# Feed-forward by Strassen's scheme: one of the seven gate and up products by a second level, the next weights asked for one tile earlier, own places for each kind of temporary

## The chip, the cores and the metric

The kernel runs on one core of one Trainium2 chip. The metric is the device time of one launch in microseconds (us); less is better. The core's engines each work through an instruction list of their own, in order: PE (TensorE, the matrix unit; its weight loads are listed apart as PEld), DVE (VectorE), ACT (ScalarE), POOL (GpSimd), and SP (SyncE), which here only asks for transfers (DMA). Engines wait for one another by semaphores. All data are float32. PE multiplies float32 words of reduced precision, so each operand is split into a high and a low word, and one product of two operands is three matmuls (high·high, high·low, low·high).

## The reference, cut to what matters

One layer (BATCH 1, SEQ 2048, D_MODEL 1024, D_FF 2816). The change touches only the last three lines:

```python
h = h + einsum(concat([fox, pool]), w_out)          # attention and pooling
h = h + einsum(mo, w_mem_out)                       # memory cross-attention
hn = rmsnorm(h, g_ffn[l])
gu = jnp.einsum('bsd,df->bsf', hn, w_gate_up[l])    # 1024 -> 2 * 2816
act = jax.nn.silu(gu[..., :D_FF]) * gu[..., D_FF:]
h = h + jnp.einsum('bsf,fd->bsd', act, w_down[l])   # 2816 -> 1024
```

## The kernel before, in words

The feed-forward part runs in two passes (`ps_` = 0, 1) over 1024 tokens each; a pass is `gate_up`, then `down`. Tokens stand in blocks of 512 (`FT`), features in tiles of 128 (`NF` = 22 tiles).

`gate_up` makes, for one tile t, gate and up of 128 features for two blocks of 512 tokens. That is a product of 2 x 2 blocks (rows: the two halves of the 1024 inputs; columns: gate and up on one side, the two token blocks on the other), done by Strassen's scheme in Winograd's form with seven products: b11·x11, b21·x12, t2·s2, t1·s1, t3·s3 in the tile's own turn, t4·x22 and b22·s4 in the turn of tile t+1. One such product (`product`) is 4 slices of 128 inputs x 3 word products = 12 matmuls of 512 columns. They gather in three PSUM banks per tile (a, b, c: banks 0 to 2 or 3 to 5 in turn); banks 6 and 7 serve the four late token tiles (below). The sums t1 to t4 of the weights are made on DVE in `weight_steps`; its `put` makes a word pair, a cast on ACT for the high word and a subtraction on DVE (line 64, `sub_hi`) for the low word. Word pairs have eight places in a ring (`word_pair`). The x and s operands of the tokens are word pairs too: x11, x12, s2, s1 stand in slabs (their tiles appear as qs, kh, kl, cb), and s3, x22, s4 are made at the start of pass 0 by `put_late` from raw loads (`xr`).

`down` multiplies the 22 activation tiles by the down weights, again with seven products, of 11 steps each: 77 steps of 12 matmuls. It draws raw blocks through SP (`draw`), splits them into word pairs (`ww`), and after a product adds four banks to four residual blocks `o` (line 1612 before, 1722 after) and stores them through POOL (`out_dram`). While it runs in pass 0, `next_ops` at steps 20, 34, 48 and 62 makes the token operands of pass 1. The sums of the down weights are made in pass 0 of `gate_up` on POOL (`down_sums`, from loads `wdr`) and written to HBM. The sums of activations are made on POOL as well (`act_sums`). Four late token tiles are normed and turned inside pass 0 of `gate_up` (`late_tile`).

Order: in the feed-forward part PE and SP go through their instructions in the order in which the code is written (`in_order(EN.SP)`). The order on DVE, ACT and POOL is set by the framework's scheduler. Blocks of temporaries come from one pool of 14 places of 128 x 512 (`temp`), and a block waits until an older holder of its place is done with.

## Time and profile before

| | |
|---|---|
| time, median of 3 runs (lowest, highest) | 2487.02 us (2485.74, 2490.58) |
| profiled execution, its own time | 2486.17 us |
| its span in the trace | 2484.4 us |
| granted TensorE clock, mean | 0.999 |
| DMA, mean over the span | 173 GB/s |
| gate_up pass 0 / down pass 0 | 1219.98 to about 1638 / to about 1852 us |
| gate_up pass 1 / down pass 1 | to about 2266 / to the end |

The rows shown below are of four kinds. A row of busy time by stretch has, behind the stretch and its length, busy us and instruction count of PE, PEld, DVE, ACT and POOL, then the granted clock (1.00 is full), the DMA share and GB/s. A row of groups has line, engine, operation, output <- inputs, shapes and count, then busy us and the mean ns of one. A row of the timeline has start, duration (of the whole run of xN), engine, line, operation, and in brackets the idle time before it with what ended it. A row of transfers has queue, count, KB each and median us from the ask to the landing. Starts are us from the start of the span. A matmul's duration is its way through the unit; the next one starts earlier.

### The profile page before, as it was taken

What the parts mean: (1) busy time and instruction counts of PE and PEld (TensorE: products, weight loads), DVE (VectorE), ACT (ScalarE), POOL (GpSimd) and SP (SyncE); (2) the same over time, 40 slices, a digit from 0 to 9 for tenths busy, and PEclk for the clock granted to TensorE, in tenths of its full rate; (3) what the DMA queues carried; (4) which work ended last, traced back from release to release, by engine and by line L of the source; (5) the groups of instructions that cost most, each with busy time, mean ns of one, the idle gap of its engine ahead of it and who ended that gap; (6) DMA issues with size and microseconds to landing.
All of it is one profiled execution on the core that took longest, in us unless ns stands there. A gap on an engine that the chain in (4) does not pass through costs nothing.

```text
span 2484.4 us, 36567 instructions
## 1 busy us (share of the span) xinstructions
PE 2468.4 (99%) x12899; PEld 2109.2 (85%) x12899; DVE 1662.4 (67%) x3000; ACT 1204.0 (48%) x2308; POOL 745.1 (30%) x1012
## 2 busy tenths in 40 slices
PE   9999999999999899999999999999999999999999
PEld 8999989878888788888888888888888888888887
DVE  7444495489999855556868787667676666665554
ACT  6434341089999835445633433335443333333443
POOL 2223200045556524343135545430002222222000
PEclk9999999999999999999999999999999999999999
DMA  8665566476776443233645544467762333325666
GB/s 295 216 191 173 163 210 180 150 197 159 177 166 156 120 149 112 106 111 134 233 158 182 193 174 167 172 230 251 259 239 98 106 119 115 107 98 198 229 204 212
DMA packets 218279, 428.95 MB, mean 173 GB/s; under 512 B 25952, under 2 KB 101728, under 8 KB 207264
## 3 DMA queue, kind: packets, MB, share of 16 engines
q1 hardware_dynamic: 187920, 330.12, 42.4%
q0 software_dynamic: 30032, 96.23, 10.4%
q8 instruction: 102, 1.67, 0.3%
q14 instruction: 81, 0.66, 0.1%
q10 hardware_dynamic: 144, 0.26, 0.0%
HBM read 287.47 MB, written 134.61 MB: 170 GB/s over the span
## 4 chain that ended last, share of the span: by engine, by line
PE 83%; DVE 1%; issue 1%; POOL 1%; ACT 0%; DVEq 0%; POOLq 0%; ACTq 0%
PE bk L71 17%; PE bk L69 17%; PE bk L70 17%; PE acc L917 5%; PE sps L841 5%; PE tp L56 4%; PE mmps L69 4%; PE mmps L71 4%; PE mmps L70 4%; PE oo L69 1%; PE oo L70 1%; PE oo L71 1%; PE zp L71 1%; PE zp L69 1%; PE zp L70 1%
## 5 line engine op out<-in xcount | busy, mean ns | idle before, releaser
L64 DVE TENSOR_TENSOR ww<-draw,ww 128x512 fp32r<-128x512 f32 x308 | 209.7, 719 | 151.1 <-ACT ww L184 150.6
L184 ACT CAST ww<-draw 128x512 fp32r<-128x512 f32 x308 | 179.2, 620 | 220.9 <-PE bk L71 175.3
L64 DVE TENSOR_TENSOR ww<-graw,ww 128x512 fp32r<-128x512 f32 x220 | 174.3, 798 | 107.8 <-ACT ww L1137 107.6
L70 PE MATMUL bk<-ww,ww 128*128 128x512 f32 x619 | 240.2, 388 | 0.0
L71 PE MATMUL bk<-ww,ww 128*128 128x512 f32 x619 | 240.2, 388 | 0.0
L69 PE MATMUL bk<-ww,ww 128*128 128x512 f32 x619 | 240.1, 388 | 0.0
L1137 ACT CAST ww<-graw 128x512 fp32r<-128x512 f32 x220 | 136.0, 622 | 179.5 <-PE bk L71 164.4
L64 DVE TENSOR_TENSOR pl<-tp,ph 128x512 fp32r<-128x512 f32 (+3 forms) x298 | 177.5, 598 | 7.3 <-ACT ph L950 6.6
L69 PE MATMUL zps<-wh,xhi 128*128 128x384 f32 (+1 forms) x512 | 174.1, 340 | 0.0
L71 PE MATMUL zps<-wh,xl 128*128 128x384 f32 (+1 forms) x512 | 172.0, 336 | 0.0
L70 PE MATMUL zps<-wl,xhi 128*128 128x384 f32 (+1 forms) x512 | 171.9, 336 | 0.0
L950 ACT CAST ph<-tp 128x512 fp32r<-128x512 f32 (+3 forms) x298 | 152.7, 529 | 24.3 <-PE tp L56 22.9
L69 PE MATMUL bk<-qs,ww 128*128 128x512 f32 x352 | 137.8, 391 | 0.0
L71 PE MATMUL bk<-qs,ww 128*128 128x512 f32 x352 | 137.2, 390 | 0.1
L70 PE MATMUL bk<-kh,ww 128*128 128x512 f32 x352 | 136.9, 389 | 0.0
L69 PE MATMUL bk<-kl,ww 128*128 128x512 f32 x352 | 136.9, 389 | 0.0
L70 PE MATMUL bk<-cb,ww 128*128 128x512 f32 x352 | 136.9, 389 | 0.0
L71 PE MATMUL bk<-kl,ww 128*128 128x512 f32 x352 | 136.9, 389 | 0.0
L71 PEld LDWEIGHTS bk<-ww,ww 128*128 128x128 f32 x619 | 116.2, 188 | 24.1
L70 PEld LDWEIGHTS bk<-ww,ww 128*128 128x128 f32 x619 | 116.2, 188 | 24.0
L69 PEld LDWEIGHTS bk<-ww,ww 128*128 128x128 f32 x619 | 116.2, 188 | 23.7
L1615 POOL DMA_DIRECT2D out_dram<-o x31 | 16.7, 541 | 374.9 <-DVE o L1612 373.0
(641 smaller groups left out, 7066.1 us busy)
## 6 DMA issues: line engine op xcount, KB each, us to landing
graw<-in_w_gu_dram SPq DMA_DIRECT2D x44, 1024.0 KB, 5.6
draw<-in_w_down_dram SPq DMA_DIRECT2D x66, 256.0 KB, 4.4
xl<-in_xT_dram SPq DMA_DIRECT2D x64, 256.0 KB, 5.5
wdr<-in_w_down_dram SPq DMA_DIRECT2D x22, 512.0 KB, 4.3
xrow<-in_x_dram SPq DMA_DIRECT2D x16, 512.0 KB, 4.8
vd<-cb SPq DMA_DIRECT2D x16, 512.0 KB, 3.6
kh<-qkT1h SPq DMA_DIRECT2D x16, 512.0 KB, 10.3
kl<-qkT1l SPq DMA_DIRECT2D x16, 512.0 KB, 12.3
```

Source lines behind the costliest of these rows:

```text
L56: return pe.transpose(out.bitcast(F32R), src, identr[:])
L64: (eng or dve).tensor_tensor(out=lo, in0=src, in1=f(hi), op=ALU.subtract)
L69: pe.matmul(ps, lhsT=sh, rhs=mh, start=first, stop=False, skip_group_check=goes_on)
L70: pe.matmul(ps, lhsT=sh, rhs=ml, start=False, stop=False, skip_group_check=goes_on)
L71: pe.matmul(ps, lhsT=sl, rhs=mh, start=False, stop=last, skip_group_check=goes_on)
L184: act.copy(hi, raw)
L841: pe.matmul(ps[:, :w], lhsT=qs[:, i * P:(i + 1) * P], rhs=kk[:, cs], start=(a == 0), stop=(a == 1))
L917: pe.matmul(acc[:m, q0 * P:], lhsT=v[:, j, :m], rhs=(pl if low else ph)[:, q0 * P:], start=state["n"] == 1, stop=state["n"] == 2 * nk)
L950: act.copy(ph[:, sl], tp[:, sl])
L1137: needs(act.copy(quad(hi), v), *(tie if nm == "t2" else ()))
L1615: pool.dma_start(out[rows_, cs], o)
```

## The change

- Tiles t-1 and t (t odd) share their b21·x12 products. Both weights times x12 are one 2 x 2 block product again, done by the same scheme one level down: seven quarter products (`quarter`) of 2 slices x 3 words = 6 matmuls of 256 columns, so 42 matmuls of 256 in place of 24 of 512. They gather in bank 7 (`u`, used three times), and in halves of two c banks. DVE adds their results to `s0` and `s1` by six adds of 256 columns and one of 512, in place of two of 512.
- `weight_steps` of an odd tile takes the b21 of both tiles (`pair`, a load of its own) and makes the seven quarter weights h11 to ht4: four more subtractions of 256 columns, and `put_half` four times (three of 512, one of 256) in place of two `put` of b21.
- x12 becomes four blocks of word pairs for the quarters (`quarter_ops`): for pass 0 after the first copy out of the first tile, for pass 1 at step 68 of `down`. s3 takes the slab of x12.
- The weights of tile t+1 are asked for at the top of tile t. In tile 0, t1·s1 comes ahead of t2·s2.
- `temp` has places for each kind (`SETS`), and a double block `tw`, which raw x12, raw s4 and the loads of the down weights share. The four `o` blocks rotate through places 0 to 7; sums and half of raw x12 have places 7 and 8.
- `down_sums` moves from POOL to DVE, by half blocks (22 calls of 4 subtractions of 256 per block). The silu of the gate works in place in PSUM. Late tiles use bank 6 only.

```diff
@@ weight_steps
+        if pair is None:
+            t4 = b[1, 0]
+            sub(t4, b[1, 0], t2)
+        else:
+            t4 = b[0, 0]
+            sub(t4, b[1, 0], t2)
+            odd = b[1, 0]
+            put_half(pair, "h11", "h21")
+            both = sum_("ht")
+            sub(both[:, :2], odd[:, :2], pair[:, :2])
+            sub(both[:, 2:], odd[:, 2:], both[:, :2])
+            put_half(both, "ht1", "ht2")
+            sub(odd[:, :2], odd[:, 2:], odd[:, :2])
+            put_half(odd, "ht3", "h22")
+            sub(pair[:, 2:], pair[:, 2:], both[:, 2:])
+            put_half(pair[:, 2:], "ht4")
@@ the feed-forward part
-        temp = lambda n: fb.tile([P, FT], F32, tag="t", name=n, bufs=14)[:]
+        SETS = dict(s1=[0, 1], s2=[2, 3, 4], s3=[5, 6], sum=[7, 8], h2=[9], x22=[3, 4, 6, 9], o=list(range(8)))
+        def temp(name, kind):
+            SETS[kind].append(SETS[kind].pop(0))
+            n = SETS[kind][-1]
+            return fb.tile([P, FT], F32, tag=f"t{n}", name=name, bufs=1)[:]
+        def raws_of(op):
+            if op == "x22":
+                return [temp("xr", "x22") for _ in range(4)]
+            t_ = wide_temp("xr")
+            return [t_[:, :FT], t_[:, FT:], temp("xr", "sum"), temp("xr", "sum")]
+        def quarter_ops(raws, *after):
...
+            def put(t_, j, v):
+                needs(act.copy(t_[:, j], v), *after)
+                sub_hi(t_[:, 2 + j], v, t_[:, j])
+            for j in range(2):
+                r0, r1 = raws[j], raws[j + 2]
+                put(first_, j, r0[:, :B])
+                put(wide[0], j, r1)
+                tt(r1[:, B:], r0[:, B:], r1[:, B:], ALU.add)
+                tt(r0[:, B:], r0[:, :B], r0[:, B:], ALU.subtract)
+                tt(r0[:, :B], r1[:, B:], r0[:, :B], ALU.subtract)
+                tt(r1[:, :B], r1[:, :B], r0[:, :B], ALU.subtract)
+                put(wide[1], j, r1)
+                put(wide[2], j, r0)
@@ down_sums
-            sub = lambda o, p_, q_: pool.tensor_tensor(out=o, in0=p_, in1=q_, op=ALU.subtract)
+            sub = lambda o, p_, q_: dve.tensor_tensor(out=o, in0=p_, in1=q_, op=ALU.subtract)
@@ gate_up
+        def quarter(ps, wop, xop, first):
+            for j in range(2):
+                cs = slice(j * P, (j + 1) * P)
+                mm3(ps, (wop[0][:, cs], wop[1][:, cs]), quarters[xop][j], first and j == 0, j == 1, not first)
+                if odd:
+                    u, c0, c1 = bank(7)[:, :B], bank(3 * ((t + 1 + turned) % 2) + 2), c[:, B:]
+                    s0 = prev["s1"]
+                    quarter(u, w["h11"], "a11", True)
+                    quarter(c1, w["ht1"], "s1", True)
+                    quarter(c0[:, :B], w["h21"], "a12", True)
+                    add(s0[:, :B], u)
+                    add(s1[:, B:], c1)
...
-                if cur:
-                    product(c, w["b21"], "x12", True)
-                    dve.tensor_tensor(out=s1, in0=c, in1=s1, op=ALU.add)
-                    act.activation(s1, s1, AF.Silu)
-                    cur["s1"] = s1
-                else:
+                if odd:
+                    quarter(u, w["ht2"], "s2", False)
+                    quarter(c1, w["h22"], "s4", False)
+                    add(s1[:, :B], u)
+                    add(s1[:, :B], c1)
+                elif not cur:
                     next(follow)
...
+                if odd:
+                    quarter(u, w["ht3"], "s3", False)
+                    quarter(c0[:, B:], w["ht4"], "a22", True)
+                    add(s0[:, B:], u)
+                    add(s1[:, B:], u)
+                    add(s0, c0)
+                    for s_ in (s0, s1):
+                        act.activation(s_, s_, AF.Silu)
@@ the call
-            early = {(0, 2): [lambda: put_late("s3")], (0, 3): [lambda: put_late("x22")], (1, 1): [lambda: put_late("s4")]}
+            early = {(0, 2): [lambda: quarter_ops(late_raw["x12"], *emptied[:1])], (0, 3): [lambda: put_late("x22")],
+                     (1, 1): [last_op]}
+            def next_quarters():
+                raws = raws_of("x12")
+                for j in range(4):
+                    sp.dma_start(raws[j], hTd[2][j + 4])
+                quarter_ops(raws)
+                between[68] = [next_quarters]
```

The first place is DVE at the end of tile 0 of pass 0. Before, three operands stand between the last low word of x22 and the low word of tile 1's b11 (`ww7_15237`; `graw` is the raw weight tile, `t1` a sum of it):

```order
L64 TENSOR_TENSOR x22l2_15141<-xr_15106,x22h2_15140 128x512 [waits DMAHW0_49,Activation_49]
L64 TENSOR_TENSOR x22l3_15143<-xr_15107,x22h3_15142 128x512 [waits DMAHW1_49,Activation_49]
L64 TENSOR_TENSOR s4l1_15123<-xr_15113,s4h1_15122 128x512 [waits DMAHW3_49,DMASW6_49,Activation_49]
L1140 TENSOR_TENSOR t1_15243<-graw_15235 128x512 [waits DMAHW0_49]
L64 TENSOR_TENSOR s4l2_15125<-xr_15114,s4h2_15124 128x512 [waits DMASW5_49,DMAHW4_49,DVE_49,Activation_49]
L64 TENSOR_TENSOR ww7_15237<-graw_15235,ww7_15237 128x512 [waits Activation_49]
```

After, the same place on DVE; `x12q` to `x12q2` are the low words of x12's quarters, line 1509 makes their sums, and `ww6_15183` is the low word of tile 1's b11:

```order
L64 TENSOR_TENSOR x12q2_15106<-xr_15052,x12q2_15106 128x512 [waits Activation_49]
L1509 TENSOR_TENSOR xr_15052<-xr_15054,xr_15052 128x256 [waits DVE_49]
L64 TENSOR_TENSOR x12q1_15105<-xr_15053,x12q1_15105 128x512 [waits Activation_49]
L1509 TENSOR_TENSOR xr_15054<-xr_15054,xr_15052 128x256 [waits DVE_49]
L64 TENSOR_TENSOR x12q2_15106<-xr_15052,x12q2_15106 128x512 [waits Activation_49]
L64 TENSOR_TENSOR x22l0_15076<-xr_15059,x22h0_15075 128x512 [waits DMASW7_49,DMAHW6_49,DMASW6_49,DMASW5_49]
L64 TENSOR_TENSOR x12q1_15105<-xr_15054,x12q1_15105 128x512 [waits Activation_49]
L64 TENSOR_TENSOR x22l1_15078<-xr_15060,x22h1_15077 128x512 [waits DMAHW7_49,DMASW1_49]
L64 TENSOR_TENSOR x22l2_15080<-xr_15061,x22h2_15079 128x512 [waits DMAHW0_49,DMASW0_49]
L64 TENSOR_TENSOR x22l3_15082<-xr_15062,x22h3_15081 128x512 [waits DMAHW1_49,DMASW4_49]
L1683 TENSOR_TENSOR s3_15178<-bk1_15088,s3_15178 128x512 [waits PE_49]
L64 TENSOR_TENSOR ww6_15183<-graw_15083,ww6_15183 128x512 [waits DMAHW2_49,Activation_49]
```

Ahead of b11 of tile 1 now stand the whole of x12's quarters, the four low words of x22, and an add that waits for the last product of tile 0.

The second place is ACT over the same tile, after the change. `s1_15102` and `s2_15156` are the copies out of bank 0 behind b11 and behind t2; the rest are high words of x12's quarters:

```order
L1627 COPY s1_15102<-bk0_15087 128x512 [waits DMASW4_49,DMASW3_49,DMAHW4_49,DMASW1_49,PE_49]
L1512 CAST x12f_15107<-xr_15052 128x256 [waits DMAHW2_49,Activation_49]
L1512 CAST x12f_15107<-xr_15052 128x256 [waits DMAHW3_49]
L1512 CAST x12q_15104<-xr_15053 128x512 [waits DMAHW4_49,DVE_49]
L1676 COPY s2_15156<-bk0_15087 128x512 [waits PE_49]
L1512 CAST x12q_15104<-xr_15054 128x512 [waits DMAHW5_49]
```

The fourth cast of x12 stands behind a copy that waits for PE's third product of tile 0.

The third place is SP at the end of the sixth product of `down` in pass 0, where a step's two raw blocks (`draw`) are asked for in pairs. Before, the blocks of steps 66, 67 and 68 stand one behind the other:

```order
L1641 DMA draw_19980<-act1b1_11413 128x512 [waits DMAHW2_49,DMAHW3_49,DMAHW1_49,DMAHW4_49,DVE_49,Activation_49]
L1642 DMA draw_19980<-wt4k0_11499 128x512
L1641 DMA draw_19980<-act3b1_11421 128x512
L1642 DMA draw_19980<-wt4k1_11503 128x512
L1641 DMA draw_20021<-act5b1_11429 128x512 [waits DMAHW6_49,DMAHW5_49,DMAHW7_49,DMAHW0_49,DVE_49]
```

After, the four raw blocks of x12 stand between them:

```order
L1752 DMA draw_20381<-wt1_11497 128x512
L1807 DMA xr_20422<-hTd2_11406 128x512 [waits DMAHW2_49]
L1807 DMA xr_20422<-hTd2_11406 128x512 [waits DMAHW3_49]
L1807 DMA xr_20423<-hTd2_11406 128x512 [waits DMAHW4_49,DMASW3_49,DVE_49]
L1807 DMA xr_20424<-hTd2_11406 128x512 [waits DMAHW5_49]
L1751 DMA draw_20457<-act5b1_11429 128x512 [waits DMAHW6_49,Activation_49]
```

The third one, `xr_20423`, goes to place 7, which the fourth `o` of the sixth product holds; its waits are for DVE's add to that block and for the block's store (`DMASW3`). The words of step 68 come from `draw_20457`, behind it. On DVE the rows from that `o` on read after the change:

```order
L1722 TENSOR_TENSOR o_19551<-bk7_19613,o_19551 128x512 [waits PE_49]
L64 TENSOR_TENSOR x12q_20429<-xr_20423,x12q_20429 128x512 [waits DMAHW4_49,Activation_49]
L1509 TENSOR_TENSOR xr_20423<-xr_20422,xr_20423 128x256 [waits DMASW3_49,DVE_49]
L64 TENSOR_TENSOR x12q_20429<-xr_20424,x12q_20429 128x512 [waits DMAHW5_49,Activation_49]
L1509 TENSOR_TENSOR xr_20422<-xr_20422 128x256 [waits DVE_49]
L1509 TENSOR_TENSOR xr_20424<-xr_20422,xr_20424 128x256 [waits DMASW7_49,DMASW4_49,DVE_49]
L1509 TENSOR_TENSOR xr_20422<-xr_20423,xr_20422 128x256 [waits DVE_49]
L1509 TENSOR_TENSOR xr_20422<-xr_20422 128x256 [waits DVE_49]
L1509 TENSOR_TENSOR xr_20423<-xr_20423,xr_20422 128x256 [waits DVE_49]
L1509 TENSOR_TENSOR xr_20422<-xr_20424,xr_20422 128x256 [waits DVE_49]
L64 TENSOR_TENSOR ww0_20458<-draw_20457,ww0_20458 128x512 [waits DMAHW6_49,Activation_49]
```

Behind these come three low words of x12, one more sum, and `ww1_20459`, the second word that step 68 needs. So the low words of step 68 stand behind nearly all of x12's quarters on DVE.

More of the change, by code (lines that the diff above doesn't have):

```diff
@@ L1495, in block_kernel @@
-        down_raw = {}
-        def load_down(k):
-            down_raw[k] = raw = wdp.tile([P, 4, FT], F32, tag="wd", name="wdr", bufs=1)
-            for c in range(2):
-                sp.dma_start(raw[:, 2 * c:2 * c + 2],
-                             w_down[:, (2 * k + c) * P:(2 * k + c + 1) * P, :].rearrange("a p c -> p a c"))
+                turn_normed(i, 4 * a, half.pop(), bank(6).rearrange("p (k t) -> p k t", k=4),
+                            hp.tile([P, 4, P], F32, tag="cm", name="hst", bufs=3))
@@ L1503, in act_sums, with down_sums @@
+        def down_sums(n):
+            k, c = divmod(n, 2)
+            raw = down_raw.pop(n)
+            b11, b12, b21, b22 = (raw[:, m] for m in range(4))
+            sub = lambda o, p_, q_: dve.tensor_tensor(out=o, in0=p_, in1=q_, op=ALU.subtract)
+            sub(b11, b12, b11)
+            sub(b12, b22, b12)
+            sub(b22, b22, b11)
+            sub(b21, b21, b22)
+            pool.dma_start(wsum[k][:, :, c * B:(c + 1) * B], raw)
         def act_sums(ps_, k, blocks, names):
@@ L1604, in residual @@
                 def residual(j):
-                    o = temp("o")
+                    o = temp("o", "o")
                     rows_, cs = place(j)
@@ L1665, in block_kernel @@
         with in_order(EN.SP):
-            for op in ("s3", "x22", "s4"):
+            for op in ("x12", "x22"):
                 load_late(op)
```

157 lines of the change are left out of this document (95 added, 62 removed).

## Prediction

> **What bounds the kernel now.** First the page: the busy line of the engines and the chain of work that ended last.
>
> ```profile
> PE 2468.4 (99%) x12899; PEld 2109.2 (85%) x12899; DVE 1662.4 (67%) x3000; ACT 1204.0 (48%) x2308; POOL 745.1 (30%) x1012
> PE 83%; DVE 1%; issue 1%; POOL 1%; ACT 0%; DVEq 0%; POOLq 0%; ACTq 0%
> ```
>
> PE is busy for 99% and carries the chain. Then busy time by stretch: gate_up of pass 0, down of pass 0, gate_up of pass 1, and 100 us of steady gate_up.
>
> ```profile
> 1220.00:1637.00 417.00, 416.91 (x1855) 344.84 (x1854) 310.99 (x365) 166.84 (x299) 186.38 (x225) 1.00 0.49 177
> 1646.00:1852.00 206.00, 206.00 (x910) 170.57 (x909) 147.00 (x224) 101.06 (x177) 20.23 (x29) 1.00 0.76 261
> 1852.00:2266.00 414.00, 414.00 (x1829) 342.79 (x1828) 260.39 (x349) 152.41 (x265) 100.17 (x126) 1.00 0.32 111
> 1500.00:1600.00 100.00, 100.00 (x442) 82.79 (x442) 73.89 (x84) 35.80 (x63) 46.02 (x54) 1.00 0.46 171
> ```
>
> PE misses 0.09 us of 417 and nothing in the rest, at full clock. So asking for weights earlier can gain nothing: there is no wait to remove. What counts is how long PE's own work gets, and whether the new work on DVE, ACT and SP makes PE wait.
>
> **Term A, PE's own work.** The matmuls of 512 columns start 100.00 / 442 = 0.226 us apart; the timeline gives 2.72 for a product of 12, which is 0.2267. Matmuls of 256 columns, each with its own weight load as here, run in the projection of `zp`. First the first matmuls of tile 0's first two products, then two stretches of `zp` alone, then one of its weight loads (ns, least/median/most):
>
> ```profile
> 1219.98 0.39 PE L69 MATMUL bk<-qs,ww 128*128 128x512 f32 x1
> 1222.70 0.39 PE L69 MATMUL bk<-kl,ww 128*128 128x512 f32 x1
> ...
> 311.00:322.00 11.00, 11.00 (x94) 11.00 (x94) 0.00 (x0) 1.00 0.91 279
> 458.50:469.00 10.50, 10.50 (x91) 10.50 (x90) 0.69 (x1) 1.00 0.69 248
> L71 PEld LDWEIGHTS zp<-xhi,wpl x256: 187/188/192, 311.0 to 469.2; 128*128 128x128 f32 x128
> ```
>
> 11.00 / 94 = 0.117 and 10.50 / 91 = 0.115. A stretch may begin and end inside a matmul, so I take 0.118, with 0.117 and 0.120 as ends. A pair of tiles loses 24 x 0.2267 = 5.44 and gets 42 x 0.118 = 4.96: 0.485 saved, for 22 pairs **-10.7 us** (-8.8 to -11.6).
>
> By the section "Back-to-back issue gap" of the Trainium skill's page "TensorE: Matmul & The Clock Gate" a lone matmul of 512 columns takes 518 cycles and one of 256 takes 262, which would be an estimated 0.59 per pair, 13.1 in all. The same section says that a real stream runs at about 131 ns for 512 columns and 81 ns for 128, which speaks against the change, as narrow matmuls would then cost more per column. The trace has 226.7 and about 117 ns, agrees with neither figure for a stream, and decides.
>
> **DVE and ACT in steady tiles.** The unit costs come from the timeline:
>
> ```profile
> 1229.33 2.49 DVE L64 TENSOR_TENSOR x22l<-xr,x22h 128x512 fp32r<-128x512 f32 x4
> 1213.08 0.69 DVE L1140 TENSOR_TENSOR t<-graw 128x512 f32<-128x512 f32 x1
> 1213.80 0.69 DVE L1140 TENSOR_TENSOR t<-graw,t 128x512 f32<-128x512 f32 x1
> L1629 DVE TENSOR_TENSOR o<-bk,o x1: 425/425/425, 2481.2 to 2481.2; 128x256 f32<-128x256 f32 x1
> 1223.90 2.18 ACT L1459 CAST s3h<-xr 128x512 fp32r<-128x512 f32 x4
> 1222.90 0.59 ACT L1534 COPY s<-bk 128x512 f32<-128x512 f32 x1 [1.76 <-PE bk L71]
> ```
>
> On DVE 512 columns cost 0.602 in a row ((2.49 - 0.69) / 3), 0.72 when one needs the one before; 256 columns take 0.425, so about 0.425 - (0.69 - 0.602) = 0.335 in a row. ACT casts in 0.52. Per pair DVE loses two adds and two low words of 512 and gets one add and three low words of 512, and eleven pieces of 256 (six adds, four subtractions, one low word): 11 x 0.335 = 3.7 us more. Eleven pairs make 41 us, and pass 1 goes from 260.39 to about 301 of 414. In pass 0 come 80 subtractions of `down_sums` (27 us), which POOL did:
>
> ```profile
> L1486 POOL TENSOR_TENSOR wdr<-wdr 128x512 f32<-128x512 f32 x30 | 42.3, 1411 | 1.2
> L64 DVE TENSOR_TENSOR ww<-graw,ww 128x512 fp32r<-128x512 f32 x107 | 96.1, 908 | 45.4 <-ACT ww L1137 45.1
> L64 DVE TENSOR_TENSOR ww<-graw,ww 128x512 fp32r<-128x512 f32 x108 | 74.9, 695 | 62.4 <-ACT ww L1137 62.4
> ```
>
> The last two rows are the same work in pass 0 (908 ns) and pass 1 (695), the first with POOL's sums beside it. Taking them off POOL gives part of that difference back, so pass 0 stays under 311 + 41 + 27 = 379 of 417. In an odd tile DVE reads `u` while PE does t4·x22 (2.72), or later b22·s4 (2.72); two adds of 256 fit there. I take 0.4 us for all late tiles and odd moments (-0.5 to 2).
>
> **Term B, the first two tiles of pass 0.** Count from F = 1219.98. PE's first four products take 4 x 2.72 = 10.88, b11 of tile 1 is wanted at 10.88, its first low word 0.45 later. Before, that low word was a trifle late:
>
> ```profile
> 1233.54 1.29 DVE L64 TENSOR_TENSOR ww<-graw,ww 128x512 fp32r<-128x512 f32 x2
> 1233.80 0.39 PE L70 MATMUL bk<-kh,ww 128*128 128x512 f32 x1
> 1234.29 0.50 PE L71 MATMUL bk<-qs,ww 128*128 128x512 f32 x1
> ```
>
> Two steps of 0.49 and 0.33 in place of 0.227: 0.37 us. After, ACT's fourth cast of x12 stands behind the copy of t2's bank: PE ends t2 at 3 x 2.72 + 0.2 = 8.36, the copy and the cast take 0.59 + 0.52, so DVE's fourth low word of x12 starts at about 9.5. From there to the low word of b11 stand eleven operations of 512 and six of 256: 11 x 0.602 + 6 x 0.335 = 8.6, and 0.6 for those that need the one before. The low word is ready at F + 18.7, so PE waits 7.4. It goes on through b11, three quarter products and t4·x22 and asks for `u` again at 25.8. But DVE still has 15 operations of 512, 5 of 256 and then the add on `u`: 18.7 + 9.0 + 1.7 + 0.4 + 1.0 for dependences = 30.8, and PE waits 4.9 more. Without waits it would have been there at 18.44. So 30.75 - 18.44 = 12.3, less the 0.37 of before: **+11.9 us** (11.1 to 15; less only if ACT's words of x12 came before the copy, which its written order excludes).
>
> **Term C, step 68 of down in pass 0.** E = 1822.60, the start of step 66:
>
> ```profile
> 1822.60 0.39 PE L69 MATMUL bk<-ww,ww 128*128 128x512 f32 x1
> ...
> 1821.35 2.48 DVE L1612 TENSOR_TENSOR o<-bk,o 128x512 f32<-128x512 f32 x4
> 1822.33 2.33 POOL L1615 DMA_DIRECT2D out_dram<-o  x4 [27.59 <-DVE o L1612]
> DMA to landing us min/median/max: 3.4/3.5/4.0
> ```
>
> The last row is of these four stores. The fourth `o` is asked out at 1822.33 + 3 x 0.6 = 1824.1 and has landed at 1827.6 = E + 5.0. Until then SP stands at x12's third load, and the draws of steps 68 to 71 behind it. The load then takes (with SP's 0.1 for the ask):
>
> ```profile
> draw<-wt4k SPq DMA_DIRECT2D x4, 256.0 KB, 3.6
> draw<-act13b SPq DMA_DIRECT2D x1, 256.0 KB, 2.8
> xraw<-hTd SPq DMA_DIRECT2D x16, 256.0 KB, 5.6
> ```
>
> I take 3.1 (few transfers are under way when SP has stood still), so L = E + 8.2. Then come ACT's cast (0.6), and on DVE, up to the second low word of step 68, seven operations of 512 and eight of 256: 4.2 + 2.7 + 0.6 for dependences = 7.5. The words are there at L + 8.1 = E + 16.3. PE wants the last of them at E + 2 x 2.72 + 0.23 = E + 5.67. **+10.6 us** (9.6 to 13.6: stores from 3.4 to 4.0, loads from 2.8 to 5.6, with and without the 0.6). DVE's queue holds nothing else that PE needs sooner. On SP the draws of the next steps are queued behind; those take 0.43 each and are off again before PE is.
>
> **Term D, the clock.** A gap of PE of some 3 us is followed by half clock:
>
> ```profile
> 860.18 0.50 PE L56 MATMUL tp<-identr,s3g 128*128 128x128 f32 x4 [2.85 <-DVE pl L64]
> 861.59 0.55 PE L917 MATMUL acc<-ph,v 128*128 128x512 f32 x1
> 865.10 0.41 PE L917 MATMUL acc<-pl,v 128*66 128x512 f32 x1
> ...
> 862.00:865.00 3.00, 3.00 (x17) 2.42 (x15) 1.75 (x4) 1.81 (x4) 0.00 (x0) 0.50 0.41 146
> ```
>
> The slow matmuls (0.55 to 0.65 for what else takes 0.41) last from 861.6 to 865.1, so half of 3.5, about 1.7 us, is lost. After B's first wait the loss falls into B's second and costs nothing; after C it counts: **+1.7 us** (0 to 3.4, as B's second wait may do the same).
>
> The same page of the Trainium skill says in "Part 1: The HAM clock gate" that an idle window of about 3.4 us halves the clock until as long a busy one; the trace agrees in the 0.50, after a gap that the record shows as 2.85.
>
> **Sum**, against the profiled execution's own 2486.17 (0.85 below the median of 2487.02): 2486.2 - 10.7 + 11.9 + 10.6 + 1.7 + 0.4 = **2500.1 us**. With all low ends it is 2495, with all high ends 2511.
>
> **Rivals.**
> 1. One of the two waits isn't there: places or queues release earlier than I read. Without C and D: 2487.8; without B: 2488.2. For it: the times are taken from an order, and a few us of slack decide; against: both follow from operations in line on one engine, whose durations vary little. No measurable change.
> 2. Faster: neither wait shows, only A: 2475.5. The mechanism is that DVE and ACT, in order but free early, have x12's words done ahead of the last product of tile 0, and the store at step 66 lands within 2 us. The point is B + C + D below 5.7 us. Against: ACT's copy stands ahead of the fourth cast, and the quickest of those stores took 3.4.
> 3. Slower still: DVE comes late in every odd tile of pass 0, because a subtraction of `down_sums` waits for its load with the adds on `u` behind it. 10 tiles by 1 to 3 us: 2510 to 2530. For: the new loads share a single block and follow each other closely; before, loads of 512 KB took this long:
>
> ```profile
> wdr<-in_w_down_dram SPq DMA_DIRECT2D x22, 512.0 KB, 4.3
> ```
>
> Against: more than 5 us (two products and more) lie between ask and use, and the new loads are half as large.
> 4. The change doesn't do what it says: 256-column matmuls are paced by the weight load of 188 ns. 42 x 0.188 - 5.44 = +2.46 per pair, so A is +54 in place of -10.7: 2565. The `zp` rows, with a load for each at 0.117, speak against it. The skill's section on issue gaps, named above, points this way with its figures for a stream.
>
> **Chances.** Forecast 0.62, first rival 0.18, second 0.10, third 0.08, fourth 0.02. The range takes in the forecast's bounds and the first rival: 2487 to 2512; the 0.20 of the others is left out. A change of 0.2% (5 us) is about what a measurement of this kernel can tell. Faster: 0.10. Within 0.2%: the first rival, 0.18, and 0.01 of the forecast's low end. Slower: 0.71.
>
> **What would show it.** A: gate_up of pass 1, free of B, gets shorter by 5.3 us, and quarter products step by 0.118. B: PE waits twice in tile 1 of pass 0, 7 and 5 us, for `ww` and for bank 7, both on DVE. C: SP stands at a load of `xr` and PE 10 us at step 68, with half clock behind it. Busy DVE in pass 0 under 380, and no PE waits in later odd tiles. If PE never waits at step 68, my reading of place 7 is wrong; if gate_up of pass 1 isn't shorter, A is.

## The result, and the profile after

Median of four runs 2525.47 us (2523.75 to 2528.07), before 2486.73 (four runs, 2485.74 to 2490.58): **1.0154 times the time before**, interval 1.0136 to 1.0171. The direction was right, the size was not: the time lies 13 us above the range. (One of the experiments, e2, ran as a whole, stages ahead of the change too, at a granted clock of 0.75, so its time can't be compared; e5 is the same kernel once more.)

The profiled execution of the changed kernel took 2528.07, the slowest of its four, with a span of 2526.4. From the page, the busy line of the engines; then busy time by stretch, one stretch for each stage, cut at the first matmul of each. Columns as before: PE, PEld, DVE, ACT, POOL, granted clock, DMA share, GB/s.

```profile
PE 2475.3 (98%) x13295; PEld 2128.3 (84%) x13295; DVE 1760.5 (70%) x3354; ACT 1226.8 (49%) x2360; POOL 680.4 (27%) x942
```

```profile
1219.89:1675.30 455.41, 434.86 (x2103) 365.76 (x2102) 359.85 (x594) 183.43 (x333) 134.02 (x170) 0.98 0.49 174
1675.30:1894.96 219.66, 208.00 (x902) 170.68 (x900) 147.61 (x237) 102.47 (x180) 12.49 (x21) 0.97 0.72 245
1894.96:2316.55 421.59, 420.87 (x2071) 357.05 (x2070) 319.69 (x476) 165.19 (x294) 103.19 (x129) 1.00 0.32 118
2316.55:2520.54 203.99, 203.99 (x909) 169.25 (x908) 111.61 (x174) 82.26 (x143) 11.47 (x20) 1.00 0.68 226
```

The same four stretches of the kernel before, cut in the same way:

```profile
1219.98:1648.52 428.54, 428.45 (x1905) 354.40 (x1904) 316.17 (x373) 171.35 (x307) 188.58 (x228) 1.00 0.49 175
1648.52:1852.53 204.01, 204.01 (x902) 168.92 (x901) 146.23 (x223) 100.45 (x176) 19.17 (x29) 1.00 0.77 263
1852.53:2276.85 424.32, 424.32 (x1874) 351.35 (x1873) 265.61 (x356) 156.38 (x272) 103.40 (x130) 1.00 0.32 111
2276.85:2480.84 203.99, 203.99 (x910) 169.26 (x908) 111.67 (x174) 82.27 (x143) 11.44 (x20) 1.00 0.67 226
```

Stage by stage the change costs +26.9, +15.7, -2.7 and 0.0 us. Another 2.2 lie behind the last matmul, so that the span grows by 42.0. Only gate_up of pass 1 got shorter. In pass 0 PE now stands still, which it did not before, and the granted clock fell with it. What PE waits for from the start of the feed-forward part on (total, times, longest):

```profile
PE bk L69 <- DVE s L1603: 13.7, 5, 4.6
PE bk L69 <- ACT ww L184: 8.0, 1, 8.0
PE bk L70 <- DVE ww L64: 3.5, 2, 3.3
PE bk L69 <- ACT ww L1138: 2.8, 1, 2.8
PE bk L71 <- DVE ww L64: 2.8, 2, 2.6
PE bk L69 <- ACT s L1676: 1.4, 2, 0.7
```

The second to fifth rows hold the waits at step 68 of `down` and at tile 1, which were forecast, the fourth as part of a wait for DVE. The first row was not: five waits for the adds on `u` (line 1603), of which the forecast had one. The other four fall between 1345 and 1520, that is in the odd tiles during which `late_tile` and `down_sums` run.

Below, **the loss in a region** is the sum of what the starts of neighbouring matmuls lie apart beyond their usual 0.227 us (0.12 for the quarters), where that is more than 0.06. It holds gaps and half clock together. After the change it is 14.0 in region B (1219 to 1260), 17.5 in region E (1260 to 1520), 14.7 in region C (1840 to 1894), 0.4 at 1678, 0.5 at 1763, and 1.0 at the start of gate_up of pass 1. Taken in the same way, the kernel before loses 0.4 in B, 0.7 in E (eight steps of 0.314 at the transposes of the late tiles, which are there after the change too) and nothing elsewhere. So the change adds 13.7 in B and 16.8 in E.

**Region E, how it comes about.** One of the four waits, in the timelines of SP, POOL, DVE and PE (start, duration, and in brackets the idle time before it and what ended it):

```profile
1367.93 0.89 SPq L1564 DMA_DIRECT2D wdr<-in_w_down_dram  x2
1364.71 0.73 POOL L1577 DMA_DIRECT2D wt<-wdr  x1 [5.08 <-DVE wdr L1572]
DMA to landing us min/median/max: 3.2/3.2/3.2
```

```profile
1363.08 1.33 DVE L1572 TENSOR_TENSOR wdr<-wdr 128x256 f32<-128x256 f32 x3
...
1372.58 0.42 DVE L1572 TENSOR_TENSOR wdr<-wdr 128x256 f32<-128x256 f32 x1 [4.51 <-DMA wdr<-in_w_down_dram]
...
1375.63 0.41 DVE L1603 TENSOR_TENSOR s<-bk,s 128x256 f32<-128x256 f32 x1
```

```profile
1376.10 0.58 PE L69 MATMUL bk<-x12q,ww 128*128 128x256 f32 x1 [4.61 <-DVE s L1603]
```

The third line is the landing of the store that POOL asked for at 1364.71: 1364.71 + 3.2 = 1367.9. Only then is the one block `tw` free, and SP asks for the next load at 1367.93. DVE stands 4.5 us at the first subtraction of that load, and the add on `u` is in line behind it. PE waits 4.6 for this add and then goes on at half clock (granted clock 0.50 from 1377 to 1381). So subtractions, store, load and subtractions follow one another in a ring through one block: a late subtraction makes the next load late, and that the next subtraction. The subtractions can come late from another side too. What DVE waits for between 1345 and 1500:

```profile
DVE wdr L1572 <- DMA wdr<-in_w_down_dram: 17.2, 7, 4.7
DVE hst L1110 <- PE bk L1107: 14.0, 3, 8.0
```

The second row is a late token tile: DVE waits for PE's transposes, with everything else behind it. The ring alone costs nothing: between 1520 and 1650, where no late tile runs, the sums go on and the loss is 0.0. Which link has to be cut is what e3, e5, e8, e10 and e11 are for.

### The profile page after: what moved, and what is told of

It is laid out like the page before. It is cut to its first block, busy times and chain, and to the rows that moved or that the text cites. A ratio compares the mean times of both kernels' runs of the same rounds, so it can differ in the third digit from the quotient of the medians.

```text
span 2526.4 us, 37892 instructions
## 1 busy us (share of the span) xinstructions
PE 2475.3 (98%) x13295; PEld 2128.3 (84%) x13295; DVE 1760.5 (70%) x3354; ACT 1226.8 (49%) x2360; POOL 680.4 (27%) x942
## 4 chain that ended last, share of the span: by engine, by line
PE 73%; issue 6%; DVE 3%; DMA 1%; POOL 1%; ACT 1%; SPq 0%; POOLq 0%; DVEq 0%; ACTq 0%
PE bk L69 14%; PE bk L70 14%; PE bk L71 14%; PE acc L917 5%; PE sps L841 5%; PE tp L56 4%; PE mmps L69 4%; PE mmps L71 3%; PE mmps L70 3%; PE oo L71 1%; PE oo L69 1%; PE oo L70 1%; DVE ww L64 1%; PE zp L71 1%; PE zp L69 1%
## 5 line engine op out<-in xcount | busy, mean ns | idle before, releaser
L1138 ACT CAST ww<-graw 128x512 fp32r<-128x512 f32 x176 | 108.3, 618 | 139.5 <-PE bk L71 131.9
L64 DVE TENSOR_TENSOR ww<-graw,ww 128x512 fp32r<-128x512 f32 x198 | 156.4, 792 | 27.4 <-ACT ww L1138 27.0
L841 PE MATMUL sps<-kh,qs 128*128 128x512 f32 (+2 forms) x320 | 124.5, 389 | 0.8 <-DVE mx L843 0.4
```

What stands on the lines that cost most here:

```text
L64: (eng or dve).tensor_tensor(out=lo, in0=src, in1=f(hi), op=ALU.subtract)
L841: pe.matmul(ps[:, :w], lhsT=qs[:, i * P:(i + 1) * P], rhs=kk[:, cs], start=(a == 0), stop=(a == 1))
L1138: needs(act.copy(quad(hi), v), *(tie if nm == "t2" else ()))
```

## The experiments

The times are those of the profiled execution; the stages are cut as above (gate_up 0 / down 0 / gate_up 1). The changed kernel has 455.4 / 219.7 / 421.6, whole 2528.1; the kernel before took 2485.6 to 2489.0 beside them. Each variant but e14 ran once. Where a variant doesn't touch a region, its loss still differs from run to run: 12.8 to 14.2 in B (e1, e3, e5, e6, e8 to e11), 16.7 to 17.6 in E (e1, e6, e7), and `down` 0 took 217.6 to 219.6 (e4, e5, e7, e8, e12). Smaller differences prove nothing.

**e1: place 7 out of the residual blocks.**

```diff
-        SETS = dict(... o=list(range(8)))
+        SETS = dict(... o=[0, 1, 2, 3, 4, 5, 6, 9])
```

> The residual blocks o get place 9 in place of place 7, so that the third raw block of x12 at step 68 finds its place free. Theory (SP stands for the store of the fourth o, then the words of step 68 stand behind x12's quarters): down of pass 0 falls from 219.7 us to 205 (it was 204.0 before the change), the whole time by about 14.7, the gaps of PE near 1855 to 1873 go. Rival (the quarters' own work on ACT and DVE, some 8 us each, holds up step 68 whatever the place): down of pass 0 stays above 211. Gate_up of pass 0 is untouched in both (455.4).

Measured 453.4 / 211.0 / 421.6, whole 2519.8. Of the 15.7 us in `down`, 8.7 went, so the store that holds place 7 was really what SP stood for. But 7.0 stay, and the result lies between the two theories, at the edge of the rival's "above 211". Even with x12 in time, DVE makes all of x12's quarters ahead of the words of step 68. If that is the rest, the wait was two in one, the place and the queue on DVE; e6 takes both away.

**e2 and e5: the sums of the down weights on POOL again** (the same kernel, run twice; only e5 can be compared).

```diff
-            sub = lambda o, p_, q_: dve.tensor_tensor(...)
+            sub = lambda o, p_, q_: pool.tensor_tensor(...)
```

> The sums of the down weights go back to POOL, all else as after the change. Theory (in the late tiles DVE stands for the load of the down weights, with the adds on u behind it): the 17 us of PE waits between 1345 and 1520 go nearly all, gate_up of pass 0 falls from 455.4 to about 440. Rival 1 (DVE is late there because it stands up to 8 us for the transposes of the late tiles): the waits stay, gate_up of pass 0 above 450. Rival 2 (POOL's sums slow DVE by sharing, as 908 against 695 ns a low word before): waits of PE spread over all odd tiles, gate_up of pass 0 no shorter than 450.

> The kernel of e2 again, since the whole of that run, stages before the change included, ran at a granted clock of 0.75. Theory (DVE stands for the loads of the down weights with the adds on u behind it): with the sums on POOL the PE waits between 1345 and 1520 fall from 17.5 us to under 4, gate_up of pass 0 from 455.4 to about 440. Rival (the stands for the late tiles' transposes make DVE late): above 450.

Measured (e5) 450.4 / 218.5 / 421.6, whole 2521.3; the loss in E fell only from 17.5 to 12.7. The waits of the ring went, but a new one came at 1486 (4.9 us between two starts), where POOL subtracts while DVE is at the weights of an odd tile. POOL and DVE there:

```profile
1484.37 3.91 POOL L1572 TENSOR_TENSOR wdr<-wdr 128x256 f32<-128x256 f32 x4
```

```profile
1485.33 1.22 DVE L1151 TENSOR_TENSOR t<-graw 128x512 f32<-128x512 f32 x1
1486.59 1.10 DVE L1151 TENSOR_TENSOR graw<-graw 128x512 f32<-128x512 f32 x1
...
1488.93 0.69 DVE L1151 TENSOR_TENSOR t<-graw,t 128x512 f32<-128x512 f32 x1
```

The last row, begun when POOL was through (1484.37 + 3.91 = 1488.28), shows what DVE takes for 512 columns alone, 0.69; beside POOL it took 1.22 and 1.10. Between 1260 and 1520, 39 of DVE's operations beside these subtractions of POOL were slowed, by some 27 us in all over 0.68 each. The result lies between the two theories: that the sums stand in DVE's line is part of the cost, but handing them back to POOL brings a cost of its own.

**e3: the subtractions behind the adds on `u`**, with the load left where it was (`added` holds the last add of each odd tile's quarters; the lines that fill it are left out here).

```diff
-            sub(b11, b12, b11)
+            needs(sub(b11, b12, b11), *added[-1:])
@@
-                early.setdefault((n + 2, 1), []).append(lambda n=n: down_sums(n))
+                early.setdefault((n + 2, 3), []).append(lambda n=n: down_sums(n))
```

> The sums of the down weights stay on DVE but are called at the end of a tile and stand behind the last add of the odd tile's quarter products. Theory (only the place of the sums in DVE's order hurts, since the adds on u stood behind them): the 17 us go, gate_up of pass 0 about 438 to 441. Rival (DVE is short of time or held by the late tiles' transposes): above 450.

A miss: 476.6 / 223.9 / 421.6, whole 2553.2. SP's waits between 1300 and 1520, then one of PE's:

```profile
SPq L1564 <- DMA wt<-wdr: 182.0, 10, 33.4
```

```profile
PE bk L1107 <- ACT h L1545: 10.2, 4, 3.9
```

Now the block is held longer still, and SP, which works in order, stands 182 us at the loads of the down weights, with the loads of `h` for the late tiles queued behind them; so PE waits for those tiles' transposes. The wait was not removed but moved from DVE to SP. The load has to move along with the subtractions, which is e11.

**e4: the low words of x22 and s4 on POOL.**

```diff
-                sub_hi(lo, late_raw[op][j], hi)
+                sub_hi(lo, late_raw[op][j], hi, pool)
```

> The low words of x22 and s4 at the start of pass 0 are made on POOL, 8 operations of 0.6 us less on DVE in the first two tiles. Theory (the two waits in tile 1 are DVE's queue alone): the low word of tile 1's b11 comes 2 us earlier and the add on u some 5 to 6 us earlier, PE's waits between 1228 and 1256 fall from 14.0 us to about 8. Rival (ACT's order or the loads set it, or POOL's sharing eats the gain): they stay within 1.5 us of 14.

Measured 450.6 / 219.6 / 421.6, whole 2522.8. The loss in B did not fall (15.1 against 14.0), and the theory that DVE's line gets shorter fell. First DVE after the change, then DVE and POOL in e4, at the same operations:

```profile
1229.99 1.43 DVE L1509 TENSOR_TENSOR xr<-xr 128x256 f32<-128x256 f32 x4
```

```profile
1229.51 4.69 DVE L1509 TENSOR_TENSOR xr<-xr 128x256 f32<-128x256 f32 x4
...
1229.47 4.11 POOL L64 TENSOR_TENSOR x22l<-xr,x22h 128x512 fp32r<-128x512 f32 x3 [8.33 <-ACT x22h L1499]
```

Four subtractions took 4.69 in place of 1.43 while POOL ran, and were through 0.6 us after POOL. One by one, the first three lasted 1.5 each in place of 0.4, and each ended 0.28 us after one of POOL's three operations. The Trainium skill's page "SBUF — State Buffer", section "Who interferes with whom", says that a DVE instruction with two SBUF inputs contends with a GpSimd instruction that reads SBUF, and that the one that comes second stands until the other is through. By that rule work that is handed from DVE to POOL costs DVE its time all the same, where both are busy; the trace agrees, with 4.69 for 1.43. (That gate_up 0 got shorter comes from E, whose loss fell to 11.7; why was not followed up.)

**e6: e1, and x12's quarters in two halves**, at steps 68 and 72 of `down`.

```diff
-            for j in range(2):
+            def half_(j):
                 r0, r1 = raws[j], raws[j + 2]
...
-                quarter_ops(raws)
+                between[72] = [quarter_ops(raws, later=True)]
```

> As e1 (own place for x12's raw blocks), and the quarters of x12 made in two halves, at steps 68 and 72. Theory after e1 (8.6 of the 15.7 us at step 68 came from the place, the other 7.0 from the quarters' work standing in one piece ahead of the words of step 68): down of pass 0 falls from e1's 211.0 to 205 to 206.5. Rival (the load of x12 itself is late, or ACT's casts hold): it stays above 209.

Measured 454.1 / 205.3 / 423.9, whole 2517.4. `down` is 1.3 us from its 204.0 of before. The second half now comes a little late for the next stage, which costs 2.3 there. So C was the place (8.7) and DVE's line (5.7), each to within some 2 us, by how far `down` 0 differs in the variants that leave it alone.

**e7: the copy of t2's bank behind the first four casts of x12** (`made` holds the casts in the order in which they are called).

```diff
+                    if t == 0 and ps_ == 0:
+                        needs(copied[-1], *made[:2], *made[4:6])
```

> In tile 0 of pass 0 ACT's copy behind t2 is held until the first four casts of x12 are done; nothing else changes by hand. Theory (DVE's chain to tile 1's b11 starts late because the fourth cast stands behind that copy; the rest is DVE's own work): DVE's low word of the fourth x12 block comes some 4 us earlier, but the next casts stand behind the copy again, so the low word of b11 comes about 1.9 us earlier and PE's waits between 1226 and 1256 fall from 14.0 to about 12. Rival (loads or DVE's other work set it): no change within 0.5 us.

Measured 454.0 / 219.1 / 421.6, whole 2527.5. The two gaps in tile 1 fell from 3.21 and 3.09 to 2.51 and 2.46 us between starts, 1.3 together. That much the copy is worth. The loss in B as a whole went from 14.0 to 12.5, but of that little is proof: it is 12.8 in e1 and e6 too, which don't touch B. In e1 no half clock follows the last gap, after the change 1.5 us of it do.

**e8: the late tiles' `hst` held behind the weights of the tile**, and the second half's transposes called later in their tile (that line is left out here).

```diff
-        dve.tensor_tensor(out=st[:], in0=tp[:], ...)
+        needs(dve.tensor_tensor(out=st[:], in0=tp[:], ...), *behind)
```

> The multiplication of a late tile's transposes (hst) is held on DVE until the weights of the tile in turn are ready, and the second half's transposes are called behind those weights; the sums of the down weights stay on DVE. Theory after e5 (DVE stands 6 to 8 us for PE's transposes at the head of its queue, with a whole tile's weights behind it; that lateness makes the sums of the down weights late, their store, the next load, and at last the adds on u): DVE's waits for transposes fall from 21 us to under 8, and PE's waits between 1345 and 1522 from 17.4 us to under 6, gate_up of pass 0 to about 444. Rival (the one block for the loads of the down weights is cause enough): they stay above 11 us.

Measured 454.1 / 217.6 / 422.5, whole 2526.2. DVE no longer waits for the transposes, and its waits for the loads are as long as ever (1345 to 1500):

```profile
DVE wdr L1574 <- DMA wdr<-in_w_down_dram: 17.8, 7, 5.3
...
DVE ht L1153 <- DMA hTd<-hst: 9.2, 4, 3.9
```

The loss in E is 16.1. The second row is new: `hst`, made later, is stored later, and DVE waits for its block instead. So the edit moved a late tile's hold on DVE and didn't take it away: a miss, which doesn't show whether the late tiles have a part in the loss. e11 says more on that.

**e9: e5, e6 and e8 together.** No new edit.

> e5, e6 and e8 in one: sums on POOL, own places and two halves for x12 at the end of down, hst behind the weights. If the parts add up: down of pass 0 205.3, gate_up of pass 1 421.6 to 423.9, gate_up of pass 0 about 442 (428.6 before, less 3.7 for the products, plus 13.7 at its start, plus 1 to 4 for what is left), the whole about 13 us over the kernel before, 2500. If POOL's sharing of DVE's time eats it, gate_up of pass 0 stays above 447.

Measured 448.5 / 204.8 / 424.9, whole 2509.2, 11.9 still lost in E: the second of the two outcomes. As in e5, what POOL takes over it takes from DVE again: between 1260 and 1520, 32 of DVE's operations beside POOL's subtractions of the down weights were slowed, by some 30 us in all over 0.68 each. In the kernel before it was 28, by some 34 us, and PE waited for none of them: slower operations on DVE don't by themselves make PE wait.

**e10: no subtractions of the down weights at all**; load and store stay. The kernel leaves out work that its result needs and serves only to read the waits.

```diff
-            sub(b11, b12, b11)
-            sub(b12, b22, b12)
-            sub(b22, b22, b11)
-            sub(b21, b21, b22)
```

> Leaves out the four subtractions of each half block of the down weights (the raw blocks are stored in their place), so DVE neither does that work nor waits for these loads; loads and stores stay. Theory (the sums on DVE, with their stand for the load, are the cause of the waits in the late tiles): PE's waits between 1345 and 1522 fall from 17.4 us to under 4, gate_up of pass 0 to about 441. Rival (DVE is late in these tiles from the quarter weights and the stands for the late tiles' transposes): over 8 us stay.

Measured 437.9 / 216.3 / 421.9, whole 2507.7. PE's busy time in the stretch from 1260 to 1520, after the change and in e10:

```profile
1260.00:1520.00 260.00, 248.40 (x1206) 209.28 (x1205) 201.78 (x336) 102.11 (x190) 86.17 (x109) 0.98 0.52 186
```

```profile
1260.00:1520.00 260.00, 259.59 (x1286) 219.77 (x1285) 197.85 (x297) 106.99 (x198) 90.79 (x117) 1.00 0.54 195
```

The loss falls from 17.5 to 1.4, of which 0.7 are the steps at the transposes. So these few operations are the cause, by their place in DVE's line or by their load. This run can't tell which: DVE's busy time falls by only 4 us, but in the same 260 us PE gets through 80 matmuls more, with the DVE work that belongs to them.

**e11: the sums kept, load and subtractions moved**: the load in the tile of the subtractions, these behind the adds.

```diff
-                early.setdefault((n + 1, 3), []).append(lambda n=n: load_down(n))
-                early.setdefault((n + 2, 1), []).append(lambda n=n: down_sums(n))
+                early.setdefault((n + 2, 1), []).append(lambda n=n: load_down(n))
+                early.setdefault((n + 2, 3), []).append(lambda n=n: down_sums(n))
@@
-            sub(b11, b12, b11)
+            needs(sub(b11, b12, b11), *added[-1:])
```

> The sums stay on DVE, behind the last add of the odd tile's quarter products as in e3, but the load is called at the start of the same tile, behind the next weights and the late tile's loads, so that SP doesn't stand at it with those behind. Theory (order alone: adds on u behind a stand for a load, and SP's stand for the store): waits between 1345 and 1522 under 5 us and no PE waits for late transposes, gate_up of pass 0 about 442. Rival (DVE has too little time in these tiles): above 448.

Measured 438.5 / 221.9 / 422.1, whole 2513.3, loss in E 2.0. The same work on the same engine, and the waits are gone: the same stretch, and what DVE waits for there most between 1345 and 1500, read

```profile
1260.00:1520.00 260.00, 259.21 (x1283) 219.34 (x1282) 213.59 (x348) 106.05 (x197) 86.90 (x116) 1.00 0.54 191
```

```profile
DVE hst L1110 <- PE bk L1107: 15.4, 3, 5.1
```

DVE is busy for 12 us more here than after the change, since the stretch holds more tiles' work, and PE hardly waits. So it is the place of the subtractions and of their load in the order, not their amount, that made PE wait. DVE still waits 15.4 us for the late tiles' transposes (14.0 after the change): such waits alone cost PE next to nothing. About 2 us come back as a longer `down` 0; the loss at its start is 4.5 in place of 0.4.

**e12: the quarters of the first pair at the end of tile 1**, and s4 made in tile 0 in place of x12's quarters, which move to tile 1.

```diff
+                held = t == 1 and ps_ == 0
-                if odd:
+                if odd and not held:
                     u, c0, c1 = ...
@@
+                if held:
+                    ... the seven quarters and their adds
-            early = {(0, 2): [lambda: quarter_ops(late_raw["x12"], *emptied[:1])], ...
+            early = {(0, 2): [lambda: put_late("s4")], ...
```

> In pass 0 the quarter products of the first pair stand at the end of tile 1 in place of its middle, s4 is made in tile 0 and x12's quarters in tile 1. Theory (the two first waits come from x12's quarters and the quarter weights standing on DVE ahead of tile 1's b11 and of the adds on u, 7 and 4 us of work more than before): PE's waits between 1226 and 1262 fall from 14.0 us to 3 to 6, gate_up of pass 0 to about 446. Rival (the loads of x12 and s4, which share one block, set the time wherever the products stand): above 10 us.

Measured 444.0 / 218.8 / 421.6, whole 2519.2. The loss in B falls from 14.0 (12.8 in e1, without half clock behind it) to 5.0. So the place of x12's quarters and of the first quarter products makes up most of B, as forecast, and the rival fell. The edit moves work on DVE and on PE at once; which of the two gave how much isn't shown.

**e13 and e14: e6, e11 and e12 in one kernel**; in e14 the loads of x12 at step 66 and its halves at 67 and 70.

```diff
-                between[72] = [quarter_ops(raws, later=True)]
+                def first_half():
+                    between[70] = [quarter_ops(raws, later=True)]
+                between[67] = [first_half]
-                between[68] = [next_quarters]
+                between[66] = [next_quarters]
```

> e6, e11 and e12 in one: x12's raw blocks with places of their own and its quarters in two halves at steps 68 and 72 of down, the sums of the down weights behind the adds, the first pair's quarter products at the end of tile 1. Theory (the three groups of waits are all of the loss, and independent): gate_up of pass 0 455.4 - 17 - 11 = 427 to 430, down of pass 0 205 to 208, gate_up of pass 1 422 to 424, the whole within 4 us of the kernel before (2483 to 2490), and not clearly faster, since waits of 1 to 5 us are left at each place. Rival (the waits only move, DVE and ACT being short of time): gate_up of pass 0 stays above 436, the whole above 2495.

> As e13, with x12's loads called at step 66 and its halves at steps 67 and 70, further from the start of the next gate_up. Same theories: gate_up of pass 1 421.6 (in place of some 424), the whole 1 to 3 us under e13, 2482 to 2488; with the rival above 2493.

e13 measured 430.5 / 213.4 / 423.9, whole 2499.6. e14, over five rounds: median **2496.65** (2495.07 to 2498.47) beside 2486.91 (2486.31 to 2488.95), ratio 1.0039 (1.0025 to 1.0052); stages 430.4 / 209.0 / 423.5. Of the 38.7 us that the change costs, 29 are won back, and the kernel before is still faster. Both are misses: expected were 2483 to 2490 for e13 and 2482 to 2488 for e14, and each lies some 9 us above its range. What PE still waits for most in e14:

```profile
PE bk L69 <- ACT s L1687: 3.1, 2, 2.5
PE bk L69 <- DVE s L1609: 1.6, 3, 0.8
PE bk L70 <- DVE ww L64: 1.5, 1, 1.5
PE bk L69 <- ACT ww L184: 1.3, 1, 1.3
```

With the clock lost behind them: 5.0 in B, 1 in E (less the 0.7 of before), 5 at the start of `down` 0, 2.9 at the start of gate_up 1, and 2.1 behind the last matmul. That is 16.0, less the 7.4 that term A gains (next section): 8.6, near the 9.7 measured. As an estimate: if all of them but the two waits for t2's copy (1.0 each) and the 2.1 at the end were to go, the time would be 2486.9 - 7.4 + 4.1 = 2483.6, 0.1% under the kernel before. That was not run.

## Why the prediction was wrong, by its own steps

| term | forecast | measured |
|---|---|---|
| A, PE's own work | -10.7 (-8.8 to -11.6) | -7.4 |
| B, tiles 0 and 1 | +11.9 (11.1 to 15) | +13.7 with 1.5 of half clock |
| C and D, step 68, clock | +10.6 + 1.7 | +14.7 with 2.6 of half clock |
| late tiles and odd moments | +0.4 (-0.5 to 2) | **+16.8** (17.5, less the 0.7 of before) |
| not in the sum | 0 | +1.9 (0.4 at 1678, 0.5 at 1763, 1.0 at the start of gate_up 1), +2.2 (end) |
| sum | +13.9 | +41.9, span +42.0 |

**The step that failed** is the one that took 0.4 us "for all late tiles and odd moments". It counted how much work DVE has there, and that bound held: DVE is busy for 359.85 us of pass 0, the forecast had "under 380". (In pass 1 the count was short, 54 us more than before in place of 41: ten of the eleven new subtractions of 256 columns on the raw weights ran beside sums on POOL and took 1.87 each, the eleventh 0.42. PE waited for none of it.) It did not follow the order in which DVE must take the work, and its own sign, "no PE waits in later odd tiles", was met by four such waits. The third rival had the mechanism, word for word a subtraction of `down_sums` that waits for its load with the adds on `u` behind it, and was given 0.08; its 2510 to 2530 us hold the measured time. What spoke against it, "more than 5 us lie between ask and use", was read from where the ask stands in the order. But SP doesn't ask there: it stands until the last store out of the same block has landed. One sum from rows of before would have shown it: a store lands after some 3.5, a load after 3 to 4, some 7 in all between one tile's last subtraction and the next tile's first, and nothing in the ring gives way where DVE is held up. e10 and e11 settle that the order and not the amount is the cause: without the subtractions 1.4 are lost, with all of them, but behind the adds and with the load moved along, 2.0. The ring itself is read from the rows of SP, POOL and DVE above. That the late tiles set it off is read from the profile too (no loss where none runs); e8 tried it and could not settle it, and e11 shows that a late tile's hold on DVE does no harm without the ring ahead of the adds.

**A** had the right mechanism and was mis-sized. In gate_up of pass 1 eleven pairs gain 421.59 - 1.0 (the one wait) - 424.32 = -3.7, 0.34 per pair in place of 0.485; the table takes it twice, for both passes. Ten steps of a quarter product, from the timeline after the change:

```profile
1251.00 0.28 PE L70 MATMUL bk<-x12q,ww 128*128 128x256 f32 x1
...
1252.20 0.37 PE L71 MATMUL bk<-x12q,ww 128*128 128x256 f32 x1
```

1.20 / 10 = 0.120, the end of the forecast's span; the mean over the 462 steps of pass 1 is 0.1195. So 42 x 0.1195 = 5.02, 0.42 saved. And the 144 matmuls of 512 columns of a pair step by 0.2273 in place of 0.2267, some 0.09. The fourth rival (paced by the weight load, 0.188) is refuted.

**B** was right: the add on `u` that PE waits for ends at F + 30.8 (F is now 1219.89), as forecast, though not every step on the way was. Its rows, the two gaps in `ww` and the one in `u`:

```profile
1234.72 0.50 PE L69 MATMUL bk<-qs,ww 128*128 128x512 f32 x1 [2.82 <-ACT ww L1138]
...
1238.15 0.79 PE L71 MATMUL bk<-qs,ww 128*128 128x512 f32 x1 [2.58 <-DVE ww L64]
...
1250.78 0.39 PE L69 MATMUL bk<-x12q,ww 128*128 128x256 f32 x1 [2.09 <-DVE s L1603]
```

The waits split otherwise than forecast (5.4 and 2.1 in place of 7.4 and 4.9), since PE ran at half clock between them and so took up part of the second, as term D said it would. In the first gap PE waits for ACT's high word of b11 before it waits for DVE's low word; the forecast had DVE alone there, and the low word came at F + 18.3, forecast F + 18.7. The 1.0 that was missed is the wait of t3 for the copy of t2's bank, 0.7 idle and a slow step: the new order of tile 0 puts the two next to each other. It comes again at the start of pass 1.

**C** was right in its place and its cause. SP, then PE:

```profile
1842.63 13.94 SPq L1807 DMA_DIRECT2D xr<-hTd  x4
```

```profile
1863.94 0.79 PE L69 MATMUL bk<-ww,ww 128*128 128x512 f32 x1 [8.04 <-ACT ww L184]
1868.02 0.80 PE L70 MATMUL bk<-ww,ww 128*128 128x512 f32 x1 [3.29 <-DVE ww L64]
```

x12's load landed 8.2 us after the start of step 66 (the prediction's E, here 1850.30), as forecast; the second low word came at E + 17.7 and not 16.3, since DVE waited 1.6 us for casts on ACT. **D** was 1.7 at one place; there are 2.6 here, 1.5 in B and more in region E, behind two of its four gaps.

The 2.2 us behind the last matmul stand in each of the variants (2.1 to 2.2, e2 apart). The traces show where they lie: POOL's closing DRAIN starts at its last store as before, but lasts 5.91 us in place of 3.08, and the rest of the end waits for it. Why it lasts longer is open.

## What to carry to other kernels

- A shared block closes a ring: work, store, landing, load, work. When a kind of temporary is given one block of its own, the time from ask to use is no longer what the written order says; count the ring, and look which instruction at its end has others in line behind it on an engine in order.
- Busy shares say what an engine can do, not when. DVE was busy for 360 of 455 us in gate_up of pass 0, and four subtractions per tile with a load to wait for, ahead of the adds instead of behind them, cost 16 us.
- If PE misses nothing before, each new wait is paid in full, and some with half clock behind it: an eighth fewer columns in one of seven products gained 7.4 us, the waits that came with it cost 47 (13.7 + 14.7 + 16.8 + 1.9).

## What of the hardware was not expected

- A gap of 2.48 us between starts (at 1248.3) was followed by eight steps of 0.427 in place of 0.227 in some profiles (after the change, e5, e7) and by none in e1. So its length alone doesn't set what a gap costs, and the sum of a region is uncertain by some 1.5 us.
- Behind the wait at 1376.1 quarters step by 0.21 at half clock, against 0.12 at full clock: a factor of 1.8, where matmuls of 512 columns go from 0.227 to 0.427, a factor of 1.9.
- Matmuls of 512 columns among the quarters step by 0.2273 rather than 0.2267; the cause was not looked for.
